# Prompt scores of a sliding-window attention: one matmul over both parts of the keys for the first block, and a vector addition

## The chip, the cores and the metric

The kernel runs on one core of a Trainium2 chip. The metric is the time of one execution on the device, in microseconds (us); the time before is the median of three runs.

## The reference

One inference step of a decoder layer for a prompt of 256 tokens and 32 sample tokens (8 sequences of 4). All 288 tokens share the weights: an input projection, a sliding-window attention with 16 query heads and 4 key heads, a gated linear attention, a merge, and a feed-forward part. What the change touches is the attention of the prompt:

```python
def sink_attend(q, k, v, mask, sink):
    s = jnp.einsum('...qkgd,...skd->...kgqs', q, k, preferred_element_type=jnp.float32) * (HEAD_DIM ** -0.5)
    s = jnp.where(mask, s, -jnp.inf)
    sk = sink.astype(jnp.float32)[:, :, None, None]
    m = jnp.maximum(jnp.max(s, axis=-1, keepdims=True), sk)
    p = jnp.exp(s - m)
    denom = jnp.sum(p, axis=-1, keepdims=True) + jnp.exp(sk - m)
    return jnp.einsum('...kgqs,...skd->...qkgd', p / denom, v.astype(jnp.float32))
```

The window is 128, so the prompt has two blocks of 128 queries. The first block sees only its own 128 keys; the second sees its own and the 128 before it. The head dimension is 64.

## The kernel before

Nearly all of the work is the multiplication of activations with weights (`gemm`, matmuls at line 260). Activations stand with features on the partitions and the 288 tokens along the free dimension. Single precision is had from three matmuls in a faster format (F32R): each weight tile `raw` of 128 x 512 is split into a high part `whi` (a cast on ScalarE, line 227) and a low part `wlo` (a subtraction on VectorE, line 167 in the helper `sub`), and the products high-high, low-high and high-low are summed in PSUM. There are five buffers each for `whi` and `wlo`, and six for the raw tiles of two such slabs that SyncE's queue loads.

Other work runs beside the gemms. Generators (`swa` for the attention, later `gla` and others) are stepped by `pump` after each chunk of a gemm, so that their instructions come between those of the gemm; a planner then puts the instructions of each engine in order, so the queues can differ from the order in the code. The part of `swa` at stake:

- The rotated keys `kv` are split into a high and a low part, `kx`, for the four key heads, each doubled onto both halves of the partitions (64 rows each).
- `scores(p, r)` handles two query heads at a time (u = 0 and 1), eight pairs in all (p of 2, r of 4). For each head, `qx` holds the high part of the queries on one half of the partitions and the low part on the other. One matmul of `qx` with `kx` high gives both query parts times the high keys; a second one with `kx` low gives the rest, summed in PSUM. This is done for two blocks: 128 queries by 128 keys, and 128 queries by 256 keys (line 483).
- Four reductions on VectorE (line 487) add the mask `maskp`, scale, write the scores to `sc` and leave the negated maximum, capped by the sink, in `nm`.
- `softmax` (lines 494 to 504) does the exponentials and the scaling on ScalarE; `turn` (line 508 on) transposes on VectorE and goes through memory; `values` (line 526) multiplies with the values.

In PSUM the three buffers `sm` of one bank each serve these small matmuls. Before, head u has its own bank: columns 0 to 127 for the first block, 128 to 383 for the second. The tile `kx` takes the places tagged "tt" and "Zb3"; after the last scores the loads of cached values (`vc`, line 550) go into the same places.

Of the kernel before, what the change touches and what calls it, by code (L numbers as in the profile page):

```python
# [13 lines left out]
F32R = mybir.dt.float32r  # L14
# [5 lines left out]
P = 128  # L20
D = 2048
KT = 16
TP = 256
# [119 lines left out]
def step_kernel(ctx: ExitStack, tc: tile.TileContext, a: dict):  # L143
    nc = tc.nc
    V, S, G, T, SY = nc.vector, nc.scalar, nc.gpsimd, nc.tensor, nc.sync
    main = ctx.enter_context(tc.tile_pool(name="main", bufs=1))
# [4 lines left out]
    def f(ap):  # L151
        return ap.bitcast(F32)

    def bank(name):
        return psm.tile([P, 512], F32, name=name, tag="sm")

    def flat(ap):
        return ap.rearrange("p a b -> p (a b)")
# [4 lines left out]
    def add(out, x, y, eng=V):  # L163
        eng.tensor_tensor(out, x, y, ALU.add)

    def sub(out, x, y, eng=V):
        eng.tensor_tensor(out, x, y, ALU.subtract)  # L167
# [249 lines left out]
    def rotate(x, tmp, rope):  # L417
        V.stream_shuffle(tmp, x, swap)
        mul(tmp, tmp, rope[:, 1])
        mul(x, x, rope[:, 0])  # L420
        add(x, x, tmp)

    def swa(pool, dram):
# [10 lines left out]
        maskp = flat(ya[:, 12:14])[:, 0:384]  # L434
# [7 lines left out]
            tmp = main.tile([P, NT], F32, name="rot", tag="zr", bufs=2)  # L442
            rotate(kv[:, p], tmp, rope)

        kx = [main.tile([P, 4, TP], F32R, name=f"kx{i}", tag=t) for i, t in ((0, "tt"), (1, "Zb3"))]
        for g in range(4):
            us, vs = slice(64 * (g % 2), 64 * (g % 2) + 64), slice(64 - 64 * (g % 2), 128 - 64 * (g % 2))
            k = kv[us, g // 2, 0:TP]
            S.copy(kx[0][us, g], k)
            S.copy(kx[0][vs, g], k)  # L450
            sub(kx[1][us, g], k, f(kx[0][us, g]))
            sub(kx[1][vs, g], k, f(kx[0][us, g]))
        for p in range(2):
            SY.dma_start(a["kp"][p], kv[:, p, P:2 * P])
            SY.dma_start(a["vp"][p], kv[:, 2 + p, P:2 * P])
# [13 lines left out]
        def scores(p, r):  # L469
            tmp = main.tile([P, NT], F32, name="rot", tag="zr", bufs=2)  # L470
            rotate(qp[p][:, r], tmp, rope)
            pr = 4 * p + r
            sc = pool.tile([P, 2, 384], F32, name="sc", tag="sc", bufs=2)
            nm = pool.tile([P, 2, 2], F32, name="nm", tag="nm", bufs=2)
            pp = [bank("score") for u in range(2)]
            for u in range(2):
                us, vs = slice(64 * u, 64 * u + 64), slice(64 - 64 * u, 128 - 64 * u)
                qx = main.tile([P, TP], F32R, name="qx", tag=("rs_m", "rs_t")[u])
                S.copy(qx[us], qp[p][us, r, 0:TP])
                sub(qx[vs], qp[p][us, r, 0:TP], f(qx[us]))  # L480
                for q0, k1 in ((0, P), (P, 2 * P)):
                    for i in range(2):
                        T.matmul(pp[u][:, q0:q0 + k1], lhsT=qx[:, q0:q0 + P], rhs=kx[i][:, 2 * p + u, 0:k1],  # L483
                                 start=i == 0, stop=i == 1)
            for u in range(2):
                for blk, sl in ((0, slice(0, P)), (1, slice(P, 384))):
                    V.tensor_tensor_reduce(out=sc[:, u, sl], in0=pp[u][:, sl], in1=maskp[:, sl], scale=-0.125,
                                           scalar=nsinkb[:, 2 * pr + u:2 * pr + u + 1], op0=ALU.add, op1=ALU.min,
                                           accum_out=nm[:, blk, u:u + 1])
            return p, pr, sc, nm  # L490
# [42 lines left out]
        for p in range(2):  # L533
            for r in range(4):
                now = scores(p, r)
                yield
                if r % 2 == 1 and len(pts) == 2:
                    values(*pts.pop(0))
                yield
                softmax(*now)  # L540
                turn(*now)
                yield
# [11 lines left out]
        sc = pool.tile([P, 4, 288], F32, name="scs", tag="scs")  # L554
# [7 lines left out]
        for pr0 in (0, 2):  # L562
            pp = [bank("scs") for _ in range(2)]
            for i in range(2):
                pr = pr0 + i
                for p in range(2):
                    for u in range(2):
                        g, us = 2 * p + u, slice(64 * u, 64 * u + 64)
# [33 lines left out]
        for pr in range(4):  # L602
            for b in range(3):
                for p in range(2):
                    for u in range(2):
                        g, rows_, ds = 2 * p + u, slice(P * (2 * p + u) + 32 * pr, P * (2 * p + u) + 32 * pr + 32), slice(64 * u, 64 * u + 64)
                        k, v = (sn[:, rows_], vn[:, p, ds]) if b == 2 else (st[:, b, rows_], vc[p][:, 2 * pr + b, ds])
                        T.matmul(po[32 * g:32 * g + 32, 64 * pr:64 * pr + 64], lhsT=k, rhs=v, start=pr == 0 and b == 0,  # L608
                                 stop=b == 2, skip_group_check=True)
        oo = pool.tile([P, 2, 4, 32], F32, name="oo", tag="sc", bufs=2)  # L610
        for p in range(2):
            for u in range(2):
                g = 2 * p + u
# [30 lines left out]
    with tc.tile_pool(name="swa", bufs=1) as spool, tc.tile_pool(name="turned", bufs=1, space=bass.MemoryType.DRAM) as turned:  # L644
        RS = (1.05,)

        ya = big("YA", "ya")
        queues[0].append(swa(spool, turned))
        gemm("q1", H, L, scaled(lambda m: qp[1][:, m]), rate=RS)
        gemm("gs0", H, L, scaled(lambda m: ya[:, m]), rate=RS)  # L650
        gemm("gs1", H, L, scaled(lambda m: ya[:, 4 + m]), rate=RS)
        gla_gemms(0, RS)
        drain(0)
# [313 lines left out]
    for j in range(4):  # L967
        sl = slice(4 * j, 4 * j + 4)
# [21 lines left out]
    for j in range(4):  # L990
        sl = slice(4 * j, 4 * j + 4)
# [4 lines left out]
    for h in range(4):  # L996
        gh[h] = rows(f"Za{(0, 2, 3, 1)[h]}", f"gh{h}", 4)
        tt = main.tile([P, 4, NT], F32, name="tt", tag="tt")
# [110 lines left out]
    parts = {}  # L1109
# [89 lines left out]
    i = 0  # L1199
    for n in (1, 1, 2, 2, 2, 2, 2, 2, 1, 1):  # L1200
        sl = slice(i, i + n)
# [89 lines left out]
```

## Time and profile before

| what | value |
|---|---|
| runs | 1720.65, 1720.71, 1725.83 us; median 1720.71 |
| the profiled execution | 1720.79 us, of which the span from first to last instruction is 1719.0 |
| PE (matmuls) | busy 1711.6 us, 13331 matmuls |
| VectorE (DVE) | busy 1230.4 us |
| ScalarE (ACT) | busy 884.5 us |
| score matmuls, line 483 | 64, between 67.7 and 141.3 us |
| DMA | 398.81 MB, mean 232 GB/s |

In the profile's rows PE stands for matmuls, PEld for the weight loads ahead of them (the stationary operand, here 128 x 128), DVE for VectorE, ACT for ScalarE, SPq for SyncE's queue. A row of a group ends with busy time, mean duration in nanoseconds, and the idle time of the engine before it. A row of the timeline begins with a start and a length in microseconds. A row of the waits reads: who waited, for whom, total in microseconds, times, longest.

### The profile page before, as it was taken

To read this page: it belongs to the slowest core of one execution; us is meant where nothing else is said; L and a number is where in the kernel's file an instruction comes from. 1 tells how busy PE (TensorE), PEld (TensorE's weight loads), DVE (VectorE), ACT (ScalarE), POOL (GpSimd) and SP (SyncE) were. 2 spreads that over 40 slices of the span, in tenths; PEclk is the share of its full clock that TensorE was granted. 3 is DMA by queue.
4 is the path that set the end of the run, shared out by engine and by line. 5 is a ranking of instruction groups with operands and counts; after the bars stand their busy time and mean duration, and the time that the engine had idled before them with its cause. 6 is when DMAs were issued, how large, how long until landed. Compare 5 with 4: busy or idle time off the path is not lost.

```text
span 1719.0 us, 34513 instructions
## 1 busy us (share of the span) xinstructions
PE 1711.6 (100%) x13331; PEld 1684.8 (98%) x13331; DVE 1230.4 (72%) x2408; ACT 884.5 (51%) x1679; POOL 3.1 (0%) x12
## 2 busy tenths in 40 slices
PE   9999999999999999999999999999999999999998
PEld 8999999999999999999999999999999999999998
DVE  8885675857757577666778777777777777768554
ACT  7675464444544555544555554455445554455543
POOL 0000000000000000000000000000000000000000
PEclk9999999999999999999999999999999999999999
DMA  8778576676676655547657777766867687776753
GB/s 291 220 221 287 183 222 250 205 237 210 219 265 189 208 198 172 181 153 272 231 204 279 249 247 275 279 227 242 293 243 273 223 275 276 248 268 220 262 168 117
DMA packets 131701, 398.81 MB, mean 232 GB/s; under 512 B 21360, under 2 KB 39728, under 8 KB 127440
## 3 DMA queue, kind: packets, MB, share of 16 engines
q1 hardware_dynamic: 130096, 393.98, 67.5%
q8 instruction: 104, 1.70, 0.4%
q10 hardware_dynamic: 1440, 2.62, 0.4%
q14 instruction: 61, 0.50, 0.1%
HBM read 360.73 MB, written 35.82 MB: 231 GB/s over the span
## 4 chain that ended last, share of the span: by engine, by line
PE 99%; DMA 1%; DVE 0%; ACT 0%; issue 0%; SPq 0%
PE mm L260 95%; PE pos L920 1%; PE mm L1186 1%; DMA raw<-in_w 1%; PE score L483 0%; PE o L526 0%; PE po L845 0%; PE po L848 0%; PE pa L773 0%; PE os L608 0%; PE scs L569 0%; PE ag L378 0%; PE po L847 0%; PE ssq L269 0%; PE pa L786 0%; PE pa L781 0%
## 5 line engine op out<-in xcount | busy, mean ns | idle before, releaser
L167 DVE TENSOR_TENSOR wlo<-raw,whi 128x512 fp32r<-128x512 f32 x1040 | 702.6, 688 | 402.2 <-ACT whi L227 399.2
L227 ACT CAST whi<-raw 128x512 fp32r<-128x512 f32 x1040 | 629.5, 618 | 701.6 <-PE mm L260 623.5
L260 PE MATMUL mm<-hh,whi 128*128 128x288 f32 x1472 | 433.5, 295 | 0.5 <-ACT whi L227 0.5
L260 PE MATMUL mm<-hl,whi 128*128 128x288 f32 x1472 | 431.2, 294 | 0.0
L260 PE MATMUL mm<-hh,wlo 128*128 128x288 f32 x1472 | 429.2, 292 | 0.1
L260 PE MATMUL mm<-ul,whi 128*128 128x288 f32 x1024 | 300.6, 294 | 0.0
L260 PE MATMUL mm<-h2l,whi 128*128 128x288 f32 x1024 | 300.6, 294 | 0.0
L260 PE MATMUL mm<-h2h,whi 128*128 128x288 f32 x1024 | 300.4, 293 | 0.0
L260 PE MATMUL mm<-uh,whi 128*128 128x288 f32 x1024 | 300.4, 293 | 0.0
L260 PE MATMUL mm<-h2h,wlo 128*128 128x288 f32 x1024 | 298.7, 292 | 0.0
L260 PE MATMUL mm<-uh,wlo 128*128 128x288 f32 x1024 | 298.7, 292 | 0.0
L260 PEld LDWEIGHTS mm<-hh,whi 128*128 128x128 f32 x1472 | 275.8, 188 | 6.5 <-ACT whi L227 3.3
L260 PEld LDWEIGHTS mm<-hh,wlo 128*128 128x128 f32 x1472 | 276.1, 188 | 0.4 <-DVE wlo L167 0.3
L260 PEld LDWEIGHTS mm<-hl,whi 128*128 128x128 f32 x1472 | 275.7, 188 | 0.0
L260 PEld LDWEIGHTS mm<-uh,wlo 128*128 128x128 f32 x1024 | 192.2, 188 | 0.0
L260 PEld LDWEIGHTS mm<-h2h,wlo 128*128 128x128 f32 x1024 | 192.2, 188 | 0.0
L260 PEld LDWEIGHTS mm<-uh,whi 128*128 128x128 f32 x1024 | 192.0, 187 | 0.0
L260 PEld LDWEIGHTS mm<-h2h,whi 128*128 128x128 f32 x1024 | 192.0, 187 | 0.0
L260 PEld LDWEIGHTS mm<-h2l,whi 128*128 128x128 f32 x1024 | 192.0, 187 | 0.0
L260 PEld LDWEIGHTS mm<-ul,whi 128*128 128x128 f32 x1024 | 192.0, 187 | 0.0
L1079 DVE SCALAR_TENSOR_TENSOR acc_s<-vb,kdk,acc_s 128x512 f32<-128x512 f32 x192 | 142.5, 746 | 0.3
L260 PE MATMUL mm<-gl,whi 128*128 128x288 f32 x256 | 75.1, 294 | 0.0
(260 smaller groups left out, 1741.0 us busy)
## 6 DMA issues: line engine op xcount, KB each, us to landing
raw<-in_w SPq DMA_DIRECT2D x518, 512.0 KB, 4.4
vb<-vd SPq DMA_DIRECT2D x32, 1024.0 KB, 6.6
raw<-in_s SPq DMA_DIRECT2D x32, 512.0 KB, 4.4
old<-in_s SPq DMA_DIRECT2D x32, 512.0 KB, 5.0
out_ssn<-old SPq DMA_DIRECT2D x32, 512.0 KB, 4.5
pd<-tb SPq DMA_DIRECT2D x32, 96.0 KB, 2.0
pt<-pd SPq DMA_DIRECT2D x8, 384.0 KB, 5.1
kept<-kept SPq DMA_DIRECT2D x6, 512.0 KB, 5.8
```

Source lines behind the costliest of these rows:

```text
L167: eng.tensor_tensor(out, x, y, ALU.subtract)
L227: S.copy(hi, raw)
L260: T.matmul(o, lhsT=(lo if j == 2 else hi)[:, sl], rhs=xl(k) if j == 1 else xh(k), start=k == 0 and j == 0, stop=k == nk - 1 and j == 2)
L920: T.matmul(pos[r:r + 32], lhsT=qm[:, t, 32 * b:32 * b + 32], rhs=st[i + g][:, 512 * t:512 * t + 512], start=b < 2, stop=b >= NB - 2)
L1079: paced(V.scalar_tensor_tensor(acc[t], v(n), k(n), acc[t], ALU.mult, ALU.add))
L1186: mm = T.matmul(pst, lhsT=k[:, blk, P * t:P * t + P], rhs=v[:, blk], start=i == 0, stop=i == 5)
```

## The change

For each key-head pair p there is now one tile `kx[p]`, with the high and the low part of both heads side by side: [128, part, head, 256 tokens]. In `scores`, the first block of each head is one matmul whose moving operand is 128 keys of the high part followed by 128 keys of the low part; their products come out side by side in 256 columns, not summed. The second block keeps its two matmuls with 256 keys, summed in PSUM. The first PSUM bank holds the first block of both heads, the second bank the second block of both. One addition on VectorE for both heads sums the low-part products of the first block and the mask into `sc`; the first block's reductions then add the high-part products to it.

```diff
-        kx = [main.tile([P, 4, TP], F32R, name=f"kx{i}", tag=t) for i, t in ((0, "tt"), (1, "Zb3"))]
+        kx = [main.tile([P, 2, 2, TP], F32R, name=f"kx{p}", tag=t) for p, t in ((0, "tt"), (1, "Zb3"))]
         for g in range(4):
             us, vs = slice(64 * (g % 2), 64 * (g % 2) + 64), slice(64 - 64 * (g % 2), 128 - 64 * (g % 2))
             k = kv[us, g // 2, 0:TP]
-            S.copy(kx[0][us, g], k)
-            S.copy(kx[0][vs, g], k)
-            sub(kx[1][us, g], k, f(kx[0][us, g]))
-            sub(kx[1][vs, g], k, f(kx[0][us, g]))
+            hi, lo = (kx[g // 2][:, i, g % 2] for i in range(2))
+            S.copy(hi[us], k)
+            S.copy(hi[vs], k)
+            sub(lo[us], k, f(hi[us]))
+            sub(lo[vs], k, f(hi[us]))
...
                 S.copy(qx[us], qp[p][us, r, 0:TP])
                 sub(qx[vs], qp[p][us, r, 0:TP], f(qx[us]))
-                for q0, k1 in ((0, P), (P, 2 * P)):
-                    for i in range(2):
-                        T.matmul(pp[u][:, q0:q0 + k1], lhsT=qx[:, q0:q0 + P], rhs=kx[i][:, 2 * p + u, 0:k1],
-                                 start=i == 0, stop=i == 1)
+                T.matmul(pp[0][:, 256 * u:256 * u + 256], lhsT=qx[:, 0:P], rhs=kx[p][:, :, u, 0:P], start=True, stop=True)
+                for i in range(2):
+                    T.matmul(pp[1][:, 256 * u:256 * u + 256], lhsT=qx[:, P:2 * P], rhs=kx[p][:, i, u], start=i == 0, stop=i == 1)
+            parts = pp[0].rearrange("p (u i k) -> p u i k", u=2, i=2)
+            add(sc[:, :, 0:P], parts[:, :, 1], maskp[:, 0:P].unsqueeze(1).broadcast_to([P, 2, P]))
             for u in range(2):
-                for blk, sl in ((0, slice(0, P)), (1, slice(P, 384))):
-                    V.tensor_tensor_reduce(out=sc[:, u, sl], in0=pp[u][:, sl], in1=maskp[:, sl], scale=-0.125,
+                for blk, sl, x, y in ((0, slice(0, P), parts[:, u, 0], sc[:, u, 0:P]),
+                                      (1, slice(P, 384), pp[1][:, 256 * u:256 * u + 256], maskp[:, P:384])):
+                    V.tensor_tensor_reduce(out=sc[:, u, sl], in0=x, in1=y, scale=-0.125,
                                            scalar=nsinkb[:, 2 * pr + u:2 * pr + u + 1], op0=ALU.add, op1=ALU.min,
                                            accum_out=nm[:, blk, u:u + 1])
```

## The prediction

> **What bounds the kernel now.** The page comes first: its span, the busy times, the forty slices and the chain of work that ended last.
>
> ```profile
> span 1719.0 us, 34513 instructions
> PE 1711.6 (100%) x13331; PEld 1684.8 (98%) x13331; DVE 1230.4 (72%) x2408; ACT 884.5 (51%) x1679; POOL 3.1 (0%) x12
> PE   9999999999999999999999999999999999999998
> DVE  8885675857757577666778777777777777768554
> PEclk9999999999999999999999999999999999999999
> PE 99%; DMA 1%; DVE 0%; ACT 0%; issue 0%; SPq 0%
> ```
>
> PE is never idle in any slice, its clock is granted in full, and the chain lies on PE for 99% of the span. So what shortens PE's own stream shortens the kernel, and what lengthens another engine costs nothing until PE has to wait for it. The scores of the prompt stand in the second to fourth slice (each 43 us). The windows view of that stretch, and the waits of PE's weight loads over the whole run:
>
> ```profile
> 65.00:144.00 79.00, 79.00 (x618) 77.76 (x617) 68.05 (x196) 56.61 (x158) 0.00 (x0) 1.00 0.70 209
> PEld mm L260 <- ACT whi L227: 3.3, 6, 0.9
> PEld mm L260 <- DVE wlo L167: 0.3, 1, 0.3
> ```
>
> The columns of the first row are length, then busy PE, PEld, DVE, ACT, POOL. PE is busy for all 79.00 us, DVE for 68.05 (86%), ACT for 56.61. The last two rows give all the waiting for split weights that PE does in the whole run: 3.3 us in six waits, the longest 0.9, for the high parts (ACT), and 0.3 us in one for the low parts (DVE).
>
> The chain of waits over the same stretch shows each pair of heads as one piece of eight matmuls. The first, a stretch of gemm after it, the second and the last:
>
> ```profile
> 67.85 0.92 PE score L483 x8
> 68.76 9.49 PE mm L260 x72
> 78.25 0.93 PE score L483 x8
> ...
> 140.67 0.92 PE score L483 x8
> ```
>
> There are eight such pieces of 0.92 to 0.93 us. The gemm's matmul (288 columns) takes 9.49/72 = 0.132 us, or 0.458 ns a column. Now the columns of a score piece: per head 2 x 128 for the first block and 2 x 256 for the second, 768; per pair 1536. By columns alone a piece would take 1536 x 0.458 = 0.703 us. About 0.215 us in each is something else.
>
> To find it I asked the timeline for PE at single instants inside the first piece. A row there begins with the start of the earliest matmul still running; the lengths overlap (pipelining), so only the starts count.
>
> ```profile
> 67.69 0.50 PE L483 MATMUL score<-kx,qx 128*128 128x128 f32 x3
> 67.75 0.44 PE L483 MATMUL score<-kx,qx 128*128 128x128 f32 x2
> 67.86 0.45 PE L483 MATMUL score<-kx,qx 128*128 128x256 f32 x2
> 68.03 0.34 PE L483 MATMUL score<-kx,qx 128*128 128x256 f32 x2
> 68.14 0.50 PE L483 MATMUL score<-kx,qx 128*128 128x128 f32 x3
> 68.20 0.44 PE L483 MATMUL score<-kx,qx 128*128 128x128 f32 x2
> 68.31 0.45 PE L483 MATMUL score<-kx,qx 128*128 128x256 f32 x2
> 68.48 0.28 PE L483 MATMUL score<-kx,qx 128*128 128x256 f32 x1
> 68.60 0.29 PE L260 MATMUL mm<-hh,whi 128*128 128x288 f32 x1
> 67.69 0.30 PEld L483 LDWEIGHTS score<-kx,qx 128*128 128x128 f32 x2
> 67.80 0.30 PEld L483 LDWEIGHTS score<-kx,qx 128*128 128x128 f32 x2
> 67.91 0.19 PEld L483 LDWEIGHTS score<-kx,qx 128*128 128x128 f32 x1
> 68.03 0.19 PEld L483 LDWEIGHTS score<-kx,qx 128*128 128x128 f32 x1
> ```
>
> Steps between starts, head by head: 0.06, 0.11, 0.17, 0.11 and 0.06, 0.11, 0.17, 0.12; together 0.91. A 128-column matmul should take 128 x 0.458 = 0.059 and a 256-column one 0.117. The first and fourth of each head do. The second and third take 0.05 too long each, so four times 0.053 = 0.21 us a piece: the missing time. The weight loads tell why: every matmul has its own, also where the same queries are used twice, and their starts are 0.11 apart and never closer. A stream of 0.06 is too short to cover a load of 0.11, so the matmul behind each 128-column one is late.
>
> **The change part by part.** *Matmuls.* The first block's two matmuls of 128 columns per head become one of 256; the second block keeps its two of 256. A pair goes from eight matmuls to six, with the same 1536 columns, and two of the eight loads go. Now every stream is 256 columns, 0.117 us, and covers the next load of 0.11: a margin of only 0.006. Six times 0.117 is 0.70 against 0.915, so 0.215 us a pair and 8 x 0.215 = 1.7 us in all.
>
> The new matmul reads its moving operand as two runs of 128, the high and the low part, 512 elements apart; the trace has no such read under these scores. The bounds: 0.117 is the fastest 256 columns have gone here. On the other side, 0.17 is the longest step of a 256-column matmul in the rows above; all six at that make 1.02 a pair, 0.1 more than now, or +0.8 us in all. A read in short runs stands in the values' matmuls (runs of 32, half of the array each):
>
> ```profile
> 103.08 1.45 PE o L526 x16
> ```
>
> Sixteen with 128 or 256 columns by halves, 3072 columns in 1.45 us: 0.47 ns a column if they go one behind the other, the gemm's price; 0.94 if two always share the array. At 0.94 the sixteen new matmuls would cost 256 x (0.94 - 0.458) = 0.124 us more each, +2.0 us, and the change as a whole +0.3. I take 0.117: the runs here are four times longer than those of 32, and the plain reading of the row says short runs cost nothing.
>
> *What the Trainium skill says of it.* "TensorE: Matmul & The Clock Gate", section "Back-to-back issue gap", gives an isolated gap of N/2.4 + 2.5 ns, which knows no weight loads: by it a piece takes 660 ns before and 655 after, and the change brings 0.04 us. The steps of 0.11 and 0.17 in the rows above contradict it for this piece. The same section's sustained figures (about 81 ns at 128 columns, 131 at 512) give by straight line 98 at 256: 716 before, 588 after, an estimate of 1.0 us gained; this trace has 0.91 before, not 0.72.
>
> *VectorE.* Each pair gets one more instruction, the add of the low scores and the mask into sc: 256 elements a partition, one operand from PSUM. The four reductions stay, with the same sizes; two read sc in place of the mask. Prices, from the groups by form:
>
> ```profile
> L487 DVE CUSTOM_DVE_ANT_0 sc<-score,ya,nsinkb 128x256 f32<-128x256 f32 x16 | 7.7, 480 | 0.0
> L167 DVE TENSOR_TENSOR qx<-swa_q,qx 64x256 fp32r<-64x256 f32 x16 | 6.7, 421 | 0.5
> L487 DVE CUSTOM_DVE_ANT_0 sc<-score,ya,nsinkb 128x128 f32<-128x128 f32 x16 | 5.5, 346 | 0.0
> ```
>
> Between 0.35 (half the elements) and 0.48 (the same number, with an accumulator) I take 0.42, the plain operation on 256. That is 8 x 0.42 = 3.4 us on DVE, from 68.05 to about 71.4 in a stretch of 77.3. Behind the add stand the reductions, whose accumulators ACT waits for, so the softmax of a pair and the weight casts behind it on ACT come up to 0.42 later. What covers this is the stock of split weights (five of each). In the first pair:
>
> ```profile
> 72.45 0.60 ACT L227 CAST whi<-raw 128x512 fp32r<-128x512 f32 x1
> 75.02 2.17 ACT L227 CAST whi<-raw 128x512 fp32r<-128x512 f32 x4
> 78.16 0.62 ACT L227 CAST whi<-raw 128x512 fp32r<-128x512 f32 x1 [0.96 <-PE mm L260]
> 76.05 2.46 DVE L167 TENSOR_TENSOR wlo<-raw,whi 128x512 fp32r<-128x512 f32 x4
> ```
>
> The cast at 78.16 waited 0.96 us for PE to leave the buffer of five casts earlier, that of 72.45. So PE reached the next one, cast at 75.02, at 78.1, and after the score piece (0.93) it needed it at 79.0. Its low part was made from 76.05, one of four in 2.46, done by 76.7: 2.3 us early. Against that stand 0.42 from the add and 0.215 from PE itself: the cover stays at 1.7. Costed at nothing; with the cover gone it would be the 3.4 us in full.
>
> *Banks.* The first bank now holds block one of both heads, the second block two. The add waits for the fourth of six matmuls where the first reduction waited for the fourth of eight; each costs nothing as long as DVE comes later than PE:
>
> ```profile
> 70.17 0.35 DVE L487 CUSTOM_DVE_ANT_0 sc<-score,ya,nsinkb 128x128 f32<-128x128 f32 x1
> ```
>
> It does, by 1.5 us after the piece was over (68.60). Behind the add on DVE queue the low parts of the weights, covered as above.
>
> *Keys.* The eight copies and eight subtractions have the same shapes, written to one tile for each pair of key heads instead of one for each part. The tile of the first two key heads ("tt") is now free after four score pieces, not eight; a later load of cached values goes there.
>
> ```profile
> SPq L550 <- PE score L483: 2.8, 1, 2.8
> L608 PEld LDWEIGHTS os<-vc,sts x64: 106/109/110, 195.4 to 199.1; 128*32 128x32 f32 x64
> ```
>
> SP's queue waits 2.8 us for the scores before that load, with weight loads behind it; the values are first read at 195.4, 50 us later. The other tile ("Zb3") is freed no sooner than now. No DMA is added. Nothing from this: ACT's casts wait for PE, not for weights from memory.
>
> *Sum.* The profiled execution took 1720.79 us, its span of 1719.0 and 1.8 around it; the median of the runs is 1720.71. 1720.8 - 1.7 + 0 = 1719.1, against the median 1719.0.
>
> **Rivals.** *The piece costs what its columns cost, or the two-run read is slow.* Either the 0.05 steps stay behind the new matmul, since the margin over the load is 0.006 us, or the runs cost what the steps saved. Between nothing gained and +0.8 by the rows' longest steps: 1720.7 to 1721.5. The short pitch of the fourth and eighth matmul, 256 behind 256, speaks against it. The isolated formula quoted from the Trainium skill lands here too.
>
> *DVE becomes the bound (slower).* The add holds up the reductions, ACT's softmax and then the casts and low parts, so PE waits at each pair. It decides where a pair's delay exceeds the cover, 2.3 us against 0.6, or where the delays add up because the stock isn't refilled in a pair; the wait of 0.96 above shows it is refilled. In full: 1719.0 + 3.4 = 1722.4.
>
> *The order shifts.* The engines' queues aren't in the code's order:
>
> ```profile
> 73.21 0.23 DVE L558 COPY qn<-swa_q 128x128 f32<-128x128 f32 x1
> ```
>
> This copy comes in the code after all eight pairs and ran in the first. One more DVE instruction can rearrange what stands behind it, here and later. Priced by the waits of PEld: if all 3.6 us went, 1715.4; if they doubled, 1722.6; eight more of the longest, 0.9, would make 1726.2.
>
> **How the numbers follow.** As forecast 0.72, with its own range of 1718.7 to 1719.4; piece unchanged or slow read 0.10; DVE bound 0.08; order shifted 0.10 (0.02 much better, 0.03 little, 0.05 much worse). The range is 1718.0 to 1722.5: it takes in the first three and leaves out the far ends of the fourth. A measurement tells about 0.3% from no change, 5.2 us. Faster by that needs the gain and nearly all the waits gone: 0.02. Slower needs 6.9 us of new waits: 0.05 of the fourth case and 0.01 of the third. Within it: 0.92.
>
> **What the profile of the changed kernel would show.** Right: 48 score matmuls in place of 64, all 128x256, pieces of 0.70 us in the chain with steps of 0.12; DVE with eight adds of 0.42 into sc; PEld's waits near 3.6 us. Wrong: steps of 0.17 or longer behind the two-run matmul; PEld waiting for wlo or whi between 65 and 144 us; another order of ACT's and DVE's work with new waits later in the run.

## The result and the profile after

The changed kernel takes 1719.54 us (median of 21 runs, 1719.03 to 1720.01). The forecast was 1719.0. The 21 runs of the kernel before, taken beside them, have a median of 1720.72; 13 of them lie between 1720.2 and 1721.0 and 8 between 1724.9 and 1725.9, and since the profiled execution (1720.79) is like the 13, the lower group, I compare with those here and below. Their median is 1720.67: 1.1 us less now, and the slowest run of the changed kernel (1720.01) is faster than the fastest of before (1720.24). The ratio over all runs, the 8 included, is 0.9985 (95% interval 0.9979 to 0.9991); the lower group's alone is 0.9993. So the gain is there, and far below the 0.3% that was taken for telling a change from none.

The page of the changed kernel, the lines that answer to those shown of before:

```profile
span 1717.9 us, 34493 instructions
PE 1710.8 (100%) x13315; PEld 1683.4 (98%) x13315; DVE 1232.1 (72%) x2416; ACT 883.8 (51%) x1679; POOL 3.1 (0%) x12
```

Sixteen matmuls fewer, eight instructions more on DVE, the span 1.1 us shorter. The chain of waits of the changed kernel, first score piece and the gemm behind it, then the last piece:

```profile
68.02 0.12 PE score L482
68.13 0.23 PE score L484 x2
68.37 0.12 PE score L482
68.48 0.24 PE score L484 x2
68.72 9.45 PE mm L260 x72
...
139.29 0.12 PE score L482
139.41 0.23 PE score L484 x2
139.64 0.11 PE score L482
139.76 0.24 PE score L484 x2
139.99 1.06 PE mm L260 x8
```

L482 is the new matmul with the high and low keys side by side, L484 the pair of the second block. From 68.02 to 68.72 the first piece takes 0.70 us where it took 0.92; each matmul takes 0.12. The last one is as short (0.70, from 139.29 to 139.99). Adding the steps between the starts of all eight pieces in the two traces gives 7.36 us before and 5.67 after: 1.69 us less, for a forecast of 1.7.

VectorE's part between 65 and 144 us, by groups; the waits between 60 and 150 us; and the windows view of 65 to 144:

```profile
L164 DVE TENSOR_TENSOR sc<-score,ya 128x256 f32<-128x256 f32 x8 | 3.4, 423 | 4.1 <-PE score L482 4.1
L490 DVE CUSTOM_DVE_ANT_0 sc<-score,sc,nsinkb 128x128 f32<-128x128 f32 x16 | 5.0, 350 | 0.0
```

```profile
DVE sc L164 <- PE score L482: 4.1, 5, 0.8
```

```profile
65.00:144.00 79.00, 79.00 (x620) 77.38 (x620) 70.80 (x207) 57.65 (x162) 0.00 (x0) 1.00 0.69 215
```

The add takes 0.42 us, eight times, 3.4 us in all. DVE's busy time in the stretch goes from 68.05 to 70.80. New is that DVE now waits for the scores, 4.1 us in five waits; PE stays at 79.00 of 79.00. The waits of the weight loads over the whole run, 3.3 and 0.3 us before, are now these, and none of them stands between 65 and 144 us:

```profile
PEld mm L260 <- ACT whi L227: 4.4, 6, 0.9
PEld mm L260 <- DVE wlo L167: 0.2, 1, 0.2
```

The order of the work moved too. In the first pair ACT's softmax began at 70.56, 1.96 us after the score piece was over (68.60); now the add begins at 68.95 and the softmax at 69.82, 1.10 after the piece (68.72):

```profile
70.56 0.40 ACT L499 ACTIVATE sc<-sc,nm 128x128 f32<-128x128 f32 x1 [1.30 <-DVE nm L487]
```

```profile
68.95 0.43 DVE L164 TENSOR_TENSOR sc<-score,ya 128x256 f32<-128x256 f32 x1
69.82 0.51 ACT L502 ACTIVATE sc<-sc,nm 128x256 f32<-128x256 f32 x1 [0.54 <-DVE nm L490]
```

The pieces gave back 1.69 us and the span only 1.14. One place where it went is the end of the attention's matmuls. The chain of the changed kernel there (L529 are the matmuls with the values), and of the kernel before:

```profile
157.37 0.80 PE o L529 x8
158.18 1.12 PE mm L260 x7
159.30 0.80 PE o L529 x8
160.10 2.45 PE mm L260 x17
```

```profile
158.99 1.45 PE o L526 x16
160.44 3.34 PE mm L260 x24
```

Sixteen matmuls in one go, 1.45 us, became two groups of eight, 1.60 us, with seven of gemm between them. The 24 of gemm take 3.57 (1.12 + 2.45) in place of 3.34. That is 0.15 + 0.23 = 0.38 us. The code of these matmuls is the same; the planner placed them otherwise. In the timeline of the changed kernel the step from the last gemm matmul into the first of these groups is 0.23 us (157.08 to 157.31), and the first gemm matmul behind it takes 0.24 (158.10 to 158.34), where gemm matmuls otherwise follow each other in 0.13: one more group means one more of each. For the other 0.18 us see the second profile of the changed kernel below.

### The profile page after: what moved, and what is told of

Read it like the earlier page. It is cut to its first block, busy times and chain, and to the rows that moved or that the text cites. A ratio compares the mean times of both kernels' runs of the same rounds, so it can differ in the third digit from the quotient of the medians.

```text
span 1717.9 us, 34493 instructions
## 1 busy us (share of the span) xinstructions
PE 1710.8 (100%) x13315; PEld 1683.4 (98%) x13315; DVE 1232.1 (72%) x2416; ACT 883.8 (51%) x1679; POOL 3.1 (0%) x12
## 4 chain that ended last, share of the span: by engine, by line
PE 99%; DMA 0%; DVE 0%; ACT 0%; issue 0%
PE mm L260 95%; PE pos L923 1%; PE mm L1189 1%; PE o L529 0%; PE po L848 0%; PE score L484 0%; DMA raw<-in_w 0%; PE po L851 0%; PE pa L776 0%; PE os L611 0%; PE scs L572 0%; PE ag L378 0%; PE score L482 0%; PE po L850 0%; PE ssq L269 0%; PE pa L789 0%
```

## The experiments

The kernel before ran beside each set of experiments. The median of its lower group moves from 1720.67 to 1720.86 us between sets, so 0.2 us between two sets says nothing.

**The new matmul split into its halves.** Undoes the merging alone; layout, banks and add stay.

```diff
-T.matmul(pp[0][:, 256 * u:256 * u + 256], lhsT=qx[:, 0:P], rhs=kx[p][:, :, u, 0:P], start=True, stop=True)
+for i in range(2):
+    T.matmul(pp[0][:, 256 * u + P * i:256 * u + P * i + P], lhsT=qx[:, 0:P], rhs=kx[p][:, i, u, 0:P], start=True, stop=True)
```

> The changed kernel with the first block's matmul of 256 columns split into its two halves of 128 again (high keys, low keys, side by side; the add and everything else stays). If the gain came from covering the weight loads: the steps of 0.06, 0.11, 0.17, 0.11 us come back, pieces of 0.91 to 0.92 us in place of 0.70 to 0.72, time about 1719.5 + 1.7 = 1721.2 us. If it came from the new banks, the layout of the keys or another order of the engines' work: pieces may be anything, but the time stays near 1719.5.

Measured: 1720.95 us (11 runs, 1720.59 to 1721.43), the time of before (1720.86, lower group of the 33 runs beside it). Its chain of waits, first piece (L483 now the two halves):

```profile
67.50 0.17 PE score L483 x2
67.67 0.28 PE score L485 x2
67.95 0.17 PE score L483 x2
68.12 0.29 PE score L485 x2
68.41 9.45 PE mm L260 x72
```

The piece is 0.91 us again. With everything else of the change in place, the gain is gone: it lies in the merging.

**Half the queries as weights, in the kernel before.** Same eight matmuls, same streams, loads of half the columns.

```diff
-T.matmul(pp[u][:, q0:q0 + k1], lhsT=qx[:, q0:q0 + P], rhs=kx[i][:, 2 * p + u, 0:k1],
+T.matmul(pp[u][0:64, q0:q0 + k1], lhsT=qx[:, q0:q0 + 64], rhs=kx[i][:, 2 * p + u, 0:k1],
```

(VectorE's reductions take 64 partitions; GpSimd sets the rest of `sc` and `nm` to zero.)

> The kernel before with only 64 of the 128 queries of each block as stationary columns in the score matmuls (half of the queries are left out; the rest of the scores are set to zero). Streams stay at 128, 128, 256, 256 columns, only the weight loads halve. If a matmul behind a 128-column one is late because its load of 0.11 us isn't covered: loads of about 0.055, steps of 0.06, 0.06, 0.12, 0.12, pieces of about 0.70 to 0.72 us and a time near 1719.0. If a short stream has a cost of its own, whatever the load: pieces stay at 0.92 and the time at 1720.7.

Measured: 1718.98 us (11 runs, 1718.69 to 1719.78). The chain; the starts of the first head's matmuls, read as in the prediction; then the loads by form, first of this kernel, then of the kernel before:

```profile
67.83 0.71 PE score L485 x8
```

```profile
67.67 0.22 PE L485 MATMUL score<-kx,qx 128*64 128x128 f32 x1
67.73 0.34 PE L485 MATMUL score<-kx,qx 128*64 128x128 f32 x2
67.78 0.40 PE L485 MATMUL score<-kx,qx 128*64 128x256 f32 x2
67.90 0.52 PE L485 MATMUL score<-kx,qx 128*64 128x256 f32 x4
```

```profile
L485 PEld LDWEIGHTS score<-kx,qx 128*64 128x64 f32 x64 | 5.9, 135 | 0.0
```

```profile
L483 PEld LDWEIGHTS score<-kx,qx 128*128 128x128 f32 x64 | 8.0, 190 | 0.0
```

The piece falls from 0.92 to 0.71 us with the matmuls as short as ever; a load takes 135 ns by the row in place of 190 (loads overlap each other in the rows, so their lengths aren't their spacing, which was 0.11 us), and the starts of a head's matmuls are 0.06, 0.06, 0.12 and 0.12 apart. So a stream of 128 columns has no cost of its own; the load behind it had. Half the weight columns are also half the rows of output, and no run here parts these two.

**The same halving in the changed kernel.** The edit is the same, on the three matmuls of a head; the add takes 64 partitions too.

```diff
-T.matmul(pp[0][:, 256 * u:256 * u + 256], lhsT=qx[:, 0:P], ...
+T.matmul(pp[0][0:64, 256 * u:256 * u + 256], lhsT=qx[:, 0:64], ...
```

> The changed kernel with only 64 of the 128 queries of each block as stationary columns in the score matmuls (half of the queries are left out; their scores are set to zero). If the streams of 256 columns already cover the loads of 0.11 us, halving the loads brings nothing: pieces of 0.70 to 0.72 us, time 1719.5. If the loads still show by their small margin, or the two-run operand costs something that the load hides: pieces move by 0.05 or more, and the time by 0.4 or more.

Measured: 1719.61 us (11 runs, 1719.20 to 1720.08), against 1719.43 for the changed kernel beside it.

```profile
67.84 0.12 PE score L484
67.96 0.23 PE score L486 x2
68.19 0.11 PE score L484
68.31 0.23 PE score L486 x2
68.53 9.49 PE mm L260 x72
```

The piece is 0.69 us against 0.70: the loads are hidden but for 0.01. This also answers the two-run operand: at 0.12 with the load out of the way and 0.12 with it, it costs nothing. All eight pieces together take 5.58 us against 5.67, too small a difference for the time to show.

**Without the add.** The first block's low-part products are left out of the scores.

```diff
-add(sc[:, :, 0:P], parts[:, :, 1], maskp[:, 0:P].unsqueeze(1).broadcast_to([P, 2, P]))
...
-(0, slice(0, P), parts[:, u, 0], sc[:, u, 0:P])
+(0, slice(0, P), parts[:, u, 0], maskp[:, 0:P])
```

> The changed kernel without VectorE's add: the low-part products of the first block are made but left out of the scores, and the reduction takes the mask. If the add is covered: the same pieces of 0.70 to 0.72 us, time 1719.0 to 1719.6, the lower end if the 0.56 us given back (1.70 less in the pieces, 1.14 less in the span) comes from the order that the add changes. If the add holds up PE: up to 3.4 us less, about 1716.

Measured: 1719.72 us (11 runs, 1719.23 to 1720.05), a little above the 1719.0 to 1719.6 of the covered case and no less than the changed kernel's time with the add. 3.4 us of VectorE bring nothing. The groups view of this kernel shows why:

```profile
L489 DVE CUSTOM_DVE_ANT_0 sc<-score,ya,nsinkb 128x128 f32<-128x128 f32 x16 | 5.6, 350 | 4.1 <-PE score L482 4.1
```

Without the add, the reduction itself waits the 4.1 us for the scores. The values' matmuls are in two groups here too, so the add isn't what splits them.

**Three more adds a pair.** Results unused, to find where the cover ends.

```diff
+for _ in range(3):
+    junk = pool.tile([P, 2, P], F32, name="junk", tag="junk")
+    add(junk, parts[:, :, 1], maskp[:, 0:P].unsqueeze(1).broadcast_to([P, 2, P]))
```

> The changed kernel with three more adds of the same kind per pair (results unused), 24 in all, some 0.37 us from start to start: about 9 us more on VectorE between 65 and 144 us, on 70.8 of 77. If the stock of split weights covers it, as for one add: a pair's softmax comes 1.1 us later against a cover of 1.7, and DVE's excess over the whole stretch, about 3 us, is below the stock of five tiles (some 6 us): PE waits 0 to 1 us more, time 1719.5 to 1720.8. If each add goes onto PE's path: 24 x 0.37 = 9 us more, 1728.

Measured: 1721.39 us (11 runs, 1720.84 to 1721.70), 1.9 more than the changed kernel. Windows view of 65 to 144 us, the added group, and PE's waits over the run:

```profile
65.00:144.00 79.00, 78.38 (x610) 76.63 (x610) 76.12 (x225) 56.19 (x156) 0.00 (x0) 1.00 0.66 207
```

```profile
L165 DVE TENSOR_TENSOR junk<-score,ya 128x256 f32<-128x256 f32 x24 | 10.0, 419 | 0.0
```

```profile
PE mm L261 <- ACT whi L228: 1.2, 2, 0.6
PE mm L261 <- DVE ya L162: 0.6, 1, 0.6
```

PE is no longer full (78.38 of 79.00) and waits 1.8 us for the two engines where the changed kernel has 0.3. The three waits of 0.6 us lie apart: one ahead of the scores, where the changed kernel has its 0.3; one at 114, in the fifth pair; one at 204. The one at 114 is the only one in the stretch, and it is not for split weights: the chain there runs through the added instructions to `ya`, DVE's product that reads a gemm result out of PSUM and comes behind them. So the cover does end, with DVE busy for 76.12 of 79 us, and at another place than the stock of `whi` and `wlo` that I had counted; 10 us more on DVE cost 1.9. The two waits from the scores on make 1.2 of it; whether the adds cause the one at 204 too is not shown. My expectation of 0 to 1 us more was too low, and 9 us much too high.

**The changed kernel again, and with the values' halves in the other order.** The second half's input is the later one; taken first, it keeps the sixteen matmuls together.

```diff
-            for i in range(2):
+            for i in (1, 0):
                 c = 256 * i
                 for cols, blk, src in ...
```

> The changed kernel as it is, run and profiled a second time beside the two others. If the part of the 0.56 us given back that lies between 202 and 258 us (gemm steps 0.7 ns slower, 0.29 us in all) is a matter of the single profiled execution, it is not there this time; if the changed order makes it, it is. The splitting of the last values' matmuls into two pieces of eight (0.80 + 0.80 us in place of 1.45, and the step behind the extra piece 0.1 longer) must be there either way. Time 1719.5.

> The changed kernel with the two halves of the values' matmuls issued in the other order, so that the half whose input comes last is first; the sixteen matmuls then stay together in the PE queue. If the split costs 0.39 us (0.15 in the values' matmuls, 0.24 in the gemm steps behind and between), one piece of 1.45 us returns and the time falls to about 1719.1. If the split costs nothing because something else ends later anyway: 1719.5.

Measured side by side: 1719.43 us (11 runs, 1719.13 to 1719.68) and 1718.86 us (11 runs, 1718.54 to 1719.42). The chain of the second:

```profile
158.96 1.45 PE o L529 x16
160.41 1.79 PE mm L260 x12
162.20 1.10 PE scs L572 x16
163.31 1.77 PE mm L260 x12
```

One piece of 1.45 us again, and the time 0.57 us lower: more than the 0.38 that the rows give, the rest not accounted for. In the first profile of the changed kernel the gemm's matmuls between 202 and 258 us follow each other in 131.7 ns on the mean, 131.1 in that of before: 0.2 us in all (the starts summed; I had 0.29). In the second profile it is 131.2, so the changed order doesn't make them slower. This version, at 1718.86, is the fastest of the kernels that compute all of the scores: 2.0 us below the 1720.86 of before (lower group of the 27 runs beside it), a ratio of 0.9988, or of 0.9976 over all 27 (0.9966 to 0.9985).

**The other parts of the change alone, and before again.** In the kernel before: the layout of the keys alone (the tiles `kx[p]` made as in the change, eight matmuls), and the use of the banks alone (the reductions read accordingly).

```diff
-rhs=kx[i][:, 2 * p + u, 0:k1]
+rhs=kx[p][:, i, u, 0:k1]
```

> The kernel before with the new layout of the keys alone (one tile for each pair of key heads, with high and low part); eight matmuls for a pair and the banks as before, no add. If the gain is the covered loads and nothing else: pieces of 0.91 to 0.93 us, the values' matmuls in one piece, time as before, 1720.7. If the earlier release of the first keys' tile is worth something: below 1720.4.

```diff
-T.matmul(pp[u][:, q0:q0 + k1], ...
+T.matmul(pp[int(q0 > 0)][:, k1 * u:k1 * u + k1], ...
```

> The kernel before with the new use of the banks alone (first block of both heads in one, second block of both in the other); eight matmuls for a pair, the keys as before, no add. If the gain is the covered loads and nothing else: pieces of 0.91 to 0.93 us and 1720.7. If the banks let the reductions and the matmuls run past each other in another way that matters: off by 0.5 us or more.

> The kernel before as it is, profiled a second time. Of its runs so far some lie near 1720.7 us and some near 1725, and none of the changed kernel's do the latter. If this execution is one of the longer ones, its trace should show in which stretch the 4.5 us lie; if it is one of the shorter, it shows how far two profiles of the same kernel differ by stretch (about 0.3 us in the first 33 us, by what the two profiles of the changed kernel showed).

Measured: 1720.25 us for the layout (11 runs, 1719.97 to 1721.23), 1720.82 for the banks (11 runs, 1720.28 to 1721.18), against 1720.72 for the lower group of before beside them. The banks bring nothing. The layout's time is 0.5 lower, below the 1720.4 that I had set for it to be worth something, with pieces as before:

```profile
68.75 0.92 PE score L484 x8
```

Where its 0.5 us lie is not shown: its profiled execution was its longest run, and by the first score piece it is already 0.8 us later than the two profiles of before (68.75 against 67.85 and 67.93). The split kernel has this layout too and still takes the time of before; it also has the values' matmuls in two groups, at 0.38 us, so the two may cancel there, which no run separates. The second profile of before is of a run of 1720.75 us, so the 4.5 us of its longer runs (6 of 12 here, 1 in 33 to 11 in 27 elsewhere) stay unexplained; no run of an edited kernel, whatever the edit, is above 1722.

## Why the prediction was right

*The matmuls.* Right in mechanism and size: 1.69 us for 1.7. The split kernel brings the time of before back, and halved loads take 1.68 us from the pieces of before without touching a stream (7.36 to 5.68, summed from the starts). The margin of 0.006 us over the load was enough. The Trainium skill's isolated gap in "TensorE: Matmul & The Clock Gate" ("Back-to-back issue gap"), by which 0.04 us were to come, leaves the loads out and did not hold for these matmuls. Its section "LDWEIGHTS (loading the stationary operand)" prices a load by its columns, by its formula an estimate of 107 ns for 128 and 53 for 64; the loads' starts 0.11 apart agree with the first, and the steps of 0.06 behind 64 columns don't contradict the second.

*The two-run operand.* Taken at 0.117 us, measured at 0.12. The upper ends (0.17, and 0.94 ns a column) did not occur. The value was right, but the reason that I gave for it from the values' matmuls was not: I read 0.47 ns a column, as if they went one behind the other. They go in pairs that start together. The rows of the kernel before, two of the values' and two of plain fp32 matmuls later in the run:

```profile
103.93 0.39 PE L526 MATMUL o<-pt,vt 128*64 128x256 f32 x2
104.15 0.39 PE L526 MATMUL o<-pt,vt 128*64 128x128 f32 x4
```

```profile
612.21 0.59 PE L847 MATMUL po<-at,vtok 128*128 128x256 f32 x2
612.64 0.38 PE L848 MATMUL po<-at,vtok 128*128 128x128 f32 x2
```

Two with 256 columns start at 103.93 and the next ones at 104.15, so a pair with 256 columns takes 0.22 us, about 0.85 ns a column and near the upper price. The matmuls of line 847 have 256 columns in one run, and two of them, one behind the other, take 0.43 us: the same 0.22 each. Both kinds have plain fp32 operands; the scores have F32R and take 0.117 for as many columns. So the high price stands with the format, in short runs and in one long run alike, and says nothing against short runs; that my misreading led to the right value was luck.

*VectorE.* Priced at 0.42 and 3.4 us, measured at 0.423 and 3.4; costed at nothing, and the kernel without it takes the same time. DVE's rise was 2.75 between 65 and 144 us where I had 71.4 to come; it is 70.80. What I had counted on, a softmax up to 0.42 us later against a cover of 1.7, is not what happened in the first pair, where the softmax came 0.86 us sooner after the piece. One remark did not hold: that DVE comes later than PE, which I showed for the first pair and took for all. It now waits 4.1 us for the scores in five of the eight. It cost nothing, as PE went on. So the nothing is shown, and the cover that was to explain it is put to the test only by the three more adds, where it ended in another way than I had reckoned.

*The keys.* Costed at nothing; the layout alone was 0.5 us faster, at a place that isn't shown.

*The rival of the order.* It came, in small: the planner split the values' matmuls, 0.38 us by the rows and 0.57 by the run that undoes it. I had given such shifts no term of the sum, only a case, priced by waits for weights; what came was more groups, not more waiting. This is the larger part of why 1719.54 stands 0.5 above the forecast, which had all 1.7 us arrive at the end; it also lies above the 1718.7 to 1719.4 that I gave the forecast case for itself. It is not the additional DVE instruction that I named: the kernel without the add has the two groups too, as has the split kernel, while the layout and the banks alone don't. Further I can't narrow it.

Two readings of the page were too strong, without weight in the sum: its digits say 90% or more for each slice of PE, and 8 in the last, not that PE is never idle; and the rows of PEld's waits leave out 0.5 us in which PE itself waited for `whi`. The sign of PEld's waits near 3.6 us came out at 4.6.

## What to carry to other kernels

When PE is full, count the time of such matmuls not by columns alone but for each as the larger of its stream and the weight load behind it. For a head here, loads of 0.11 us and streams of 0.06, 0.06, 0.12 and 0.12, that is 0.11 + 0.11 + 0.12 + 0.12, or 0.92 a pair, as measured. A stream shorter than the load behind it made the next matmul late, even where both use the same weights. Putting two short streams of the same stationary operand side by side, and summing elsewhere, pays as long as another engine has room, and stops paying once the stream covers the load. Look at the order of the queues after such a change; up to a third of the gain was lost in matmuls that the change didn't touch, and one line got it back.

## What was not expected of the hardware

A group of the values' matmuls put between those of the gemm costs more than its own time: 0.1 us going in and 0.1 coming out, where the scores' pieces cost neither (the timeline has 0.13 us on both sides of the first one before). Two profiles of the changed kernel differ by 0.49 us before the first score piece (68.02 against 67.53 us), which is as much as the smaller effects here; only the starts inside a piece, which repeat to 0.01 us, were fit for judging the change.
